# Where the low parts of two mixers' weights are computed, and where a softmax is scaled: VectorE and GpSimd change work

## The chip, the cores and the metric

The kernel runs on one core of a Trainium2 chip. The metric is the device time of one execution in microseconds (us). The matrix engine is called TensorE or PE, its weight loads PEld, VectorE DVE, ScalarE ACT, GpSimd POOL, and SyncE (which only issues DMAs here) SP. The granted clock is the share of TensorE's full speed that the chip allowed in a stretch; the two levels of the clock are 1.2 and 2.4 GHz.

## The reference

Two layers over 512 tokens of width 1024, float32. Layer 0 mixes tokens with two kinds of softmax attention side by side (a dilated window attention with 12 heads whose groups are combined, and a latent attention with 12 heads); layer 1 with a state-space recurrence (16 heads, in chunks of 128 tokens) beside a stick-breaking attention of 8 heads. Each is followed by a gated feed-forward block.

```python
def reference(x, positions, ...):
    for i in range(DEPTH):                       # DEPTH = 2, x is [1, 512, 1024]
        h = rmsnorm(x, mix_norms[i])
        if i % 2 == 0:
            x = x + even_mixer(h, positions, *mixers[i])
        else:
            x = x + odd_mixer(h, *mixers[i])
        x = x + conv_ffn(rmsnorm(x, ffn_norms[i]), *ffns[i])
    return rmsnorm(x, final_norm)

# in even_mixer, for every head and block of 128 queries
probs = jax.nn.softmax(jnp.where(causal, scores, -jnp.inf), axis=-1)
...
return jnp.einsum('bhqk,bkhd->bqhd', probs.astype(v.dtype), v)

def conv_ffn(h, w_gate, w_up, conv_w, conv_b, w_down):      # 1024 -> 2816 -> 1024
    gate = causal_dwconv(h @ w_gate, conv_w, conv_b)
    return (jax.nn.silu(gate) * (h @ w_up)) @ w_down
```

## The kernel before

Features lie on the partitions and the 512 tokens along the free dimension. TensorE multiplies in a rounded float32 format, so each float32 operand is split into a high part (the rounded copy) and a low part (what the rounding left), and a product is three matmuls: high by high, high by low, low by high.

**The weights.** They stream from memory in chunks of 128 partitions by up to 1024 columns. `wchunk` (L209 to L218) does one chunk: a DMA issued by SP into `wraw` (two buffers), the high part `whi` by ACT (L215), and the low part `wlo` = `wraw` - `whi` (L217), two buffers each. Unless its argument `eng` names an engine, L217 runs on GpSimd. `wstack` (L220 to L234) does the same for narrow weights, its low part at L233. The first two chunks are written out in `build` (L383). A buffer comes free when TensorE has multiplied with the chunk that was in it.

**The stages.** `build` runs four phases one after the other: mixer 0 (`even_mixer`), the feed-forward block 0, mixer 1 (`odd_mixer`: the state-space part `ssd`, then the stick-breaking part), the feed-forward block 1 with the final norm. The work that depends only on weights (projections) is cut into pieces by a `Stream`, and the pieces are put between the steps of the heads, so that TensorE has something to do while VectorE and ScalarE work on a head. TensorE takes its instructions in the order of the program; for the other engines a scheduler fixes the order when the kernel is built. Each engine then takes its own instructions strictly in that order.

**A head of mixer 0.** Per block of queries, TensorE writes the scores `s`, then `softmax` takes the maximum (L572, VectorE), the exponential with its sum (L575, ACT), the reciprocal `rl` of the sum (L576, VectorE) and multiplies by it (L577, VectorE; blocks of 128 to 512 keys, 64 in all). TensorE transposes the result (`t`), which is again split (`pth` on ACT, `ptl` on VectorE, L595 and L948), and multiplies it with the values (`o`). Before the heads, queries and keys are rotated (`rot`, `sw`, L726 to L731), split (`qk`, L261) or, for the latent attention, computed from the latents (`lat`, low part `ll`, L693; keys `knp` with low part `kl`, L850 and L868).

**The start.** The squares of x are computed on ACT and GpSimd (`sq`, L648) and added on VectorE (L652), between the first weights.

**The state-space part.** `run_conv` convolves a projection (`gt`, `cv`, L1144); `prepare` (L1260 to L1280) multiplies x by the time step (`xd`, L1269, alternately on GpSimd and VectorE), splits it (`xdt`, L1274), applies the skip term and the decay on GpSimd (L1277, L1279); `cdec` (L1258) is the decay of a chunk; `weights` computes a head's matrix and splits it (`sg`, L1328; `mh`, L261), and `apply` multiplies.

## Time and profile before

| | us |
|---|---|
| time, median of 3 runs | 1495.36 (1494.40 to 1495.47) |
| span of the profiled execution | 1491.7 |
| median less that span | 3.7 |
| PE busy | 1423.6 |
| PEld busy (beside PE) | 1158.3 |
| DVE busy | 874.7 |
| POOL busy | 697.1 |
| ACT busy | 658.0 |

The span is the time from the first to the last instruction in the profile of one execution; the time that is measured around an execution is some microseconds longer. TensorE is busy for 95% of the span, and its busy time includes matmuls that run at the low clock. The five stages of the span are mixer 0 (0 to 347 us), feed-forward 0 (347 to 712), the state-space part of mixer 1 (712 to 935), its stick-breaking part (935 to 1117), and feed-forward 1 with the end (1117 to 1492).

### The profile page before, as it was taken

Reading aid. Unit: us, or ns where it says so; the run is one execution under the profiler, and the core shown is the slowest. Engines: PE = TensorE matmul, PEld = TensorE weight load, DVE = VectorE, ACT = ScalarE, POOL = GpSimd, SP = SyncE. Lnnn points to the kernel's source line nnn. Section 1 sums busy time; section 2 is a strip of 40 time slices with the busy share of each in tenths; the row PEclk is TensorE's granted clock in tenths of the full one; section 3 lists DMA queues with packets and bytes.
Section 4 is the critical chain, followed back from the end, with each engine's and each line's share of the span. In section 5 each row is a group of like instructions: output and inputs, shape, how many; then the busy total and the mean of one; then the engine's idle time right before and its main releaser. Section 6 shows DMA issues by size and latency. Waiting matters only on the chain.

```text
span 1491.7 us, 18087 instructions
## 1 busy us (share of the span) xinstructions
PE 1423.6 (95%) x6842; PEld 1158.3 (78%) x6842; DVE 874.7 (59%) x1332; ACT 658.0 (44%) x1071; POOL 697.1 (47%) x405
## 2 busy tenths in 40 slices
PE   7989999999999999999988898999999999999997
PEld 5777778787888888888866667777888888888886
DVE  7888678736555555121788987678436555553123
ACT  4456456534433333232565465567444333333232
POOL 3633334133655555444335641466555555555441
PEclk8999999999999999999999999999999999999999
DMA  4321122122332233333222011111132233323332
GB/s 149 110 67 55 60 66 69 38 66 85 93 95 97 99 99 95 92 103 92 76 70 71 29 58 43 45 58 43 40 115 87 99 100 99 99 93 98 90 104 96
DMA packets 40006, 120.80 MB, mean 81 GB/s; under 512 B 5232, under 2 KB 8560, under 8 KB 39920
## 3 DMA queue, kind: packets, MB, share of 16 engines
q1 hardware_dynamic: 38160, 117.92, 25.1%
q10 hardware_dynamic: 1760, 1.73, 0.4%
q8 instruction: 54, 0.88, 0.2%
q14 instruction: 32, 0.26, 0.1%
HBM read 114.39 MB, written 2.10 MB: 78 GB/s over the span
## 4 chain that ended last, share of the span: by engine, by line
PE 77%; DVE 16%; ACT 3%; issue 3%; DMA 1%; POOL 0%; DVEq 0%; SPq 0%; ACTq 0%; POOLq 0%
PE proj L109 47%; PE o L109 19%; PE z L109 5%; PE s L109 3%; DVE cv L1144 2%; PE t L112 2%; PE t L109 1%; DVE mh L261 1%; DVE kl L868 1%; ACT whi L215 1%; DVE sg L1328 1%; DVE s L577 1%; DVE ptl L595 0%; DVE xe L261 0%; DVE s L572 0%
## 5 line engine op out<-in xcount | busy, mean ns | idle before, releaser
L217 POOL TENSOR_TENSOR wlo<-wraw,whi 128x1024 fp32r<-128x1024 f32 (+3 forms) x215 | 500.1, 2326 | 545.0 <-ACT whi L215 545.0
L215 ACT ACTIVATE whi<-wraw 128x1024 fp32r<-128x1024 f32 (+3 forms) x219 | 222.0, 1015 | 368.4 <-PE proj L109 320.4
L109 PE MATMUL proj<-xh,whi 128*128 128x512 f32 x844 | 348.5, 413 | 8.1 <-ACT xh L326 6.1
L109 PE MATMUL proj<-xh,wlo 128*128 128x512 f32 x844 | 336.8, 399 | 3.5 <-DVE wlo L383 3.3
L109 PE MATMUL proj<-xl,whi 128*128 128x512 f32 x844 | 336.6, 399 | 0.6 <-DVE xl L327 0.6
L109 PE MATMUL proj<-act,whi 128*128 128x512 f32 (+1 forms) x748 | 219.3, 377 | 0.0
L109 PEld LDWEIGHTS proj<-xh,whi 128*128 128x128 f32 x844 | 162.9, 193 | 45.5 <-ACT xh L326 8.8
L109 PEld LDWEIGHTS proj<-xh,wlo 128*128 128x128 f32 x844 | 162.4, 192 | 40.2 <-DVE wlo L383 3.7
L109 PEld LDWEIGHTS proj<-xl,whi 128*128 128x128 f32 x844 | 163.0, 193 | 30.8 <-DVE xl L327 2.3
L109 PEld LDWEIGHTS proj<-act,whi 128*128 128x128 f32 x748 | 137.6, 188 | 25.8
L109 PE MATMUL o<-xh,wlo 128*128 128x512 f32 x368 | 143.4, 390 | 0.0
L109 PE MATMUL o<-xh,whi 128*128 128x512 f32 x368 | 143.3, 389 | 0.0
L109 PE MATMUL o<-xl,whi 128*128 128x512 f32 x368 | 143.2, 389 | 0.0
L109 PE MATMUL proj<-act,wlo 128*128 128x512 f32 (+1 forms) x374 | 140.8, 376 | 0.0
L362 DVE TENSOR_TENSOR x<-x,proj 128x512 f32<-128x512 f32 x31 | 21.2, 685 | 177.2 <-PE proj L109 177.2
L515 DVE SCALAR_TENSOR_TENSOR cv<-gt,cols,cv 128x511 f32<-128x511 f32 x44 | 94.3, 2147 | 35.9 <-ACT cv L514 35.9
L519 POOL TENSOR_TENSOR sl<-sl,rsr 128x512 f32<-128x512 f32 x44 | 57.8, 1313 | 94.2 <-ACT sl L518 94.2
L524 DVE TENSOR_TENSOR up<-sl,o 128x512 f32<-128x512 f32 x44 | 30.3, 688 | 91.8 <-POOL sl L519 91.8
L518 ACT ACTIVATE sl<-cv 128x512 f32<-128x512 f32 x44 | 27.8, 631 | 127.3 <-DVE cv L516 127.3
L261 DVE TENSOR_TENSOR act<-up,act 128x512 fp32r<-128x512 f32 x44 | 63.2, 1436 | 29.3 <-ACT act L260 29.3
L109 PEld LDWEIGHTS proj<-act,wlo 128*128 128x128 f32 x374 | 70.4, 188 | 12.9
L109 PEld LDWEIGHTS o<-xh,wlo 128*128 128x128 f32 x368 | 69.1, 188 | 14.4
(302 smaller groups left out, 2232.4 us busy)
## 6 DMA issues: line engine op xcount, KB each, us to landing
wraw<-in_g SPq DMA_DIRECT2D x44, 512.0 KB, 3.5
wraw<-in_u SPq DMA_DIRECT2D x44, 512.0 KB, 3.4
wraw<-in_d SPq DMA_DIRECT2D x32, 448.0 KB, 3.2
wraw<-in_wqk SPq DMA_DIRECT2D x20, 512.0 KB, 3.5
wraw<-in_d SPq DMA_DIRECT2D x17, 512.0 KB, 3.5
wraw<-in_wx SPq DMA_DIRECT2D x12, 512.0 KB, 3.5
wraw<-in_wv SPq DMA_DIRECT2D x10, 512.0 KB, 3.5
wraw<-in_wz SPq DMA_DIRECT2D x8, 512.0 KB, 3.4
```

The costliest lines, as they stand in the source:

```text
L109: return self._put(self.b.nc.tensor.matmul(*args, **kw))
L112: return self._put(self.b.nc.tensor.transpose(*args))
L215: nc.scalar.activation(hi[:, :n], raw[:, :n], AF.Copy)
L217: (eng or nc.gpsimd).tensor_tensor(lo[:, :n], raw[:, :n], hi[:, :n].bitcast(F32), op=ALU.subtract)
L261: nc.vector.tensor_tensor(lo, src, hi.bitcast(F32), op=ALU.subtract)
L362: self.nc.vector.tensor_tensor(self.x[m], self.x[m], ps, op=ALU.add)
L515: nc.vector.scalar_tensor_tensor(c[:, 1:], gt[:, : T - 1], col_(1), c[:, 1:], op0=ALU.mult, op1=ALU.add)
L518: nc.scalar.activation(s, c, AF.Silu)
L519: nc.gpsimd.tensor_tensor(s, s, r, op=ALU.mult)
L524: nc.vector.tensor_tensor(u, s, pu, op=ALU.mult)
L577: nc.vector.tensor_scalar(t, t, rl, None, op0=ALU.mult)
L1144: nc.vector.scalar_tensor_tensor(c[:, d:], gt[:, : T - d], col_(j), c[:, d:], op0=ALU.mult, op1=ALU.add)
```

## The change

Two edits. In both mixers the low parts of the weights (L217, L233) are computed by VectorE, in both feed-forward blocks by GpSimd as before: an attribute `self.lo` holds the engine, and `build` sets it ahead of each phase. And in `softmax` the multiplication by 1/l is GpSimd's. The lines of the changed kernel behind `build`'s first phase carry numbers that are higher by five.

```diff
@@ wchunk
         lo = self.wp.tile([P, 1024], F32R, tag="wlo", name=self.nm("wlo"))
-        (eng or nc.gpsimd).tensor_tensor(lo[:, :n], raw[:, :n], hi[:, :n].bitcast(F32), op=ALU.subtract)
+        (eng or self.lo).tensor_tensor(lo[:, :n], raw[:, :n], hi[:, :n].bitcast(F32), op=ALU.subtract)
         return hi, lo
@@ wstack
-        nc.gpsimd.tensor_tensor(w[:, :, l0:l1], raw, w[:, :, a:b].bitcast(F32), op=ALU.subtract)
+        self.lo.tensor_tensor(w[:, :, l0:l1], raw, w[:, :, a:b].bitcast(F32), op=ALU.subtract)
         return w
@@ build
+        self.lo = nc.vector
         with self.phase("l0", s=2, t=2, o=2) as pool:
             self.even_mixer(pool)
+        self.lo = nc.gpsimd
         with self.phase("f0", t=2, o=2) as pool:
...
+        self.lo = nc.vector
         with self.tc.tile_pool(name="l1", bufs=1) as pool:
             self.odd_mixer(pool)
+        self.lo = nc.gpsimd
         with self.phase("f1", t=2, o=2) as pool:
@@ softmax
         nc.vector.reciprocal(rl, l)
-        nc.vector.tensor_scalar(t, t, rl, None, op0=ALU.mult)
+        nc.gpsimd.tensor_scalar(t, t, rl, None, op0=ALU.mult)
         return t
```

Over the whole program 82 low parts go from GpSimd's row to VectorE's: in mixer 0 20 of 1024 columns, 8 of 896, 6 of 768 and one stack of 512; in mixer 1 34 of 1024, 8 of 768, 4 of 512 and one stack of 128. The 64 multiplications of the softmax go the other way: 24 of 512 columns, 16 of 384, 12 of 256 and 12 of 128. The rows of TensorE and of SP stay as they were. Three places show what VectorE's and GpSimd's rows look like.

**The start of mixer 0.** VectorE's row before, from the sums of squares to the first angles:

```order
L664 CAST posf<-posi 128x512
L652 TENSOR_TENSOR sq_150<-sq_150,sq_166 128x512
L383 TENSOR_TENSOR wlo_79<-wraw_77,whi_78 128x512
L652 TENSOR_TENSOR sq_152<-sq_152,sq_163 128x512
L546 TENSOR_SCALAR ang_256<-posf,freq 128x512
L652 TENSOR_TENSOR sq_152<-sq_152,sq_169 128x512
L547 TENSOR_SCALAR angk_257<-ang_256 128x512
```

and now, with a second piece from the steps of the reciprocal root (`rst`, `rsy`):

```order
L657 TENSOR_TENSOR sq_150<-sq_150,sq_166 128x512
L383 TENSOR_TENSOR wlo_79<-wraw_77,whi_78 128x512
L657 TENSOR_TENSOR sq_152<-sq_152,sq_163 128x512
L551 TENSOR_SCALAR ang_256<-posf,freq 128x512
L217 TENSOR_TENSOR wlo_176<-wraw_172,whi_174 128x1024
L657 TENSOR_TENSOR sq_152<-sq_152,sq_169 128x512
...
L272 TENSOR_TENSOR rst_240<-rsy_239 128x4
L273 SCALAR_TENSOR_TENSOR rst_240<-rst_240,rsv_237 128x4
L274 SCALAR_TENSOR_TENSOR rsy_239<-rst_240,rsy_239 128x4
L217 TENSOR_TENSOR wlo_390<-wraw_386,whi_388 128x1024
L272 TENSOR_TENSOR rst_240<-rsy_239 128x4
```

The low part `wlo_176` now stands ahead of the last of these sums, and `wlo_390` among the steps of the reciprocal root. On GpSimd both stood behind the squares.

**The first scores of a head.** GpSimd's row before, from the first weight of this stretch to the second rotation's end:

```order
L217 TENSOR_TENSOR wlo_538<-wraw_534,whi_536 128x768
L730 TENSOR_TENSOR sw_496<-sw_496,sin 128x512
L731 TENSOR_TENSOR rot_497<-rot_497,sw_496 128x512
L217 TENSOR_TENSOR wlo_590<-wraw_586,whi_588 128x1024
L730 TENSOR_TENSOR sw_576<-sw_576,sin 128x512
L731 TENSOR_TENSOR rot_577<-rot_577,sw_576 128x512
L217 TENSOR_TENSOR wlo_645<-wraw_641,whi_643 128x768
L217 TENSOR_TENSOR wlo_747<-wraw_743,whi_745 128x1024
L730 TENSOR_TENSOR sw_733<-sw_733,sin 128x512
```

and now:

```order
L735 TENSOR_TENSOR sw_496<-sw_496,sin 128x512
L736 TENSOR_TENSOR rot_497<-rot_497,sw_496 128x512
L735 TENSOR_TENSOR sw_576<-sw_576,sin 128x512
L736 TENSOR_TENSOR rot_577<-rot_577,sw_576 128x512
L582 TENSOR_SCALAR s_126_656<-s_126_656,st_655 128x512
L582 TENSOR_SCALAR s_129_670<-s_129_670,st_669 128x384
L582 TENSOR_SCALAR s_132_684<-s_132_684,st_683 128x256
L582 TENSOR_SCALAR s_135_698<-s_135_698,st_697 128x128
L735 TENSOR_TENSOR sw_733<-sw_733,sin 128x512
```

The four low parts have left, and the multiplications of the softmax stand between two of the rotations (`sw`, `rot`). VectorE's row now, in the same stretch:

```order
L774 TENSOR_TENSOR rt_611<-proj_604,qt_520 128x512
L873 TENSOR_TENSOR kl_568<-knp_602,kh_567 64x512
L873 TENSOR_TENSOR kl_572<-knp_602,kh_571 64x512
L628 TENSOR_TENSOR v_622<-t_617,v_622 128x8x64
L774 TENSOR_TENSOR rt_632<-proj_625,qt_524 128x512
L261 TENSOR_TENSOR qk_614<-rt_611,qk_613 128x512
L217 TENSOR_TENSOR wlo_645<-wraw_641,whi_643 128x768
L261 TENSOR_TENSOR qk_635<-rt_632,qk_634 128x512
L577 ISA s_126_656,st_655<-s_651,masks 128x512
```

Here `wlo_645` has come in between the low parts `qk` of the first head's queries and keys, ahead of the first softmax (the row that reads the scores `s_651`).

**The values of the state-space part.** VectorE's row before, from the last convolution on:

```order
L1138 TENSOR_TENSOR gt_6699<-proj_6668,rsr_6080 128x512
L1269 TENSOR_TENSOR xd_6759<-xs_6087,tok 128x512
L1144 SCALAR_TENSOR_TENSOR cv_6701<-gt_6699,cols,cv_6701 128x511
L1144 SCALAR_TENSOR_TENSOR cv_6701<-gt_6699,cols,cv_6701 128x510
L1144 SCALAR_TENSOR_TENSOR cv_6701<-gt_6699,cols,cv_6701 128x509
L1258 COPY cdec<-s_6739 128x48
L1274 TENSOR_TENSOR xdt_6747<-xd_6745,xdt_6747 128x4x64
L1274 TENSOR_TENSOR xdt_6750<-xd_6745,xdt_6750 128x4x64
```

and now:

```order
L1143 TENSOR_TENSOR gt_6699<-proj_6668,rsr_6080 128x512
L217 TENSOR_TENSOR wlo_6718<-wraw_6714,whi_6716 128x1024
L1274 TENSOR_TENSOR xd_6759<-xs_6087,tok 128x512
L1149 SCALAR_TENSOR_TENSOR cv_6701<-gt_6699,cols,cv_6701 128x511
L1279 TENSOR_TENSOR xdt_6747<-xd_6745,xdt_6747 128x4x64
L1279 TENSOR_TENSOR xdt_6750<-xd_6745,xdt_6750 128x4x64
L1149 SCALAR_TENSOR_TENSOR cv_6701<-gt_6699,cols,cv_6701 128x510
L1279 TENSOR_TENSOR xdt_6761<-xd_6759,xdt_6761 128x4x64
L1279 TENSOR_TENSOR xdt_6764<-xd_6759,xdt_6764 128x4x64
L1263 COPY cdec<-s_6739 128x48
```

GpSimd's row at the same place before:

```order
L217 TENSOR_TENSOR wlo_6718<-wraw_6714,whi_6716 128x1024
L1269 TENSOR_TENSOR xd_6745<-xs_6087,tok 128x512
L1277 TENSOR_TENSOR xs_6087<-xs_6087,dbc 128x512 x2
L1279 TENSOR_TENSOR xd_6745<-xd_6745,tok 128x512
L1279 TENSOR_TENSOR xd_6759<-xd_6759,tok 128x512
L217 TENSOR_TENSOR wlo_6840<-wraw_6836,whi_6838 128x1024
L1269 TENSOR_TENSOR xd_6773<-xs_6087,tok 128x512
```

and now:

```order
L1274 TENSOR_TENSOR xd_6745<-xs_6087,tok 128x512
L1282 TENSOR_TENSOR xs_6087<-xs_6087,dbc 128x512 x2
L1284 TENSOR_TENSOR xd_6745<-xd_6745,tok 128x512
L1284 TENSOR_TENSOR xd_6759<-xd_6759,tok 128x512
L1274 TENSOR_TENSOR xd_6773<-xs_6087,tok 128x512
```

On VectorE the low part `wlo_6718` stands ahead of `xd_6759`, and `cdec`, which stood ahead of the four `xdt`, now stands behind them and ahead of the convolution's last step. On GpSimd nothing stands ahead of `xd_6745` and `xd_6773` but work on the same values.

## Rows read from the trace of the kernel before

**Rows 1.** The profile's page: the line of the span, the busy time of each engine (us, share of the span, instructions), and each engine's share of the chain that ended last.

```profile
span 1491.7 us, 18087 instructions
PE 1423.6 (95%) x6842; PEld 1158.3 (78%) x6842; DVE 874.7 (59%) x1332; ACT 658.0 (44%) x1071; POOL 697.1 (47%) x405
...
PE 77%; DVE 16%; ACT 3%; issue 3%; DMA 1%; POOL 0%; DVEq 0%; SPq 0%; ACTq 0%; POOLq 0%
```

**Rows 2.** Busy time by stage; a row is a stretch in us from the span's start (mixer 0; FFN 0; the state-space part of mixer 1; its stick-breaking part). Columns: length, the busy time of PE, PEld, DVE, ACT and POOL with the number of instructions, the granted clock of TensorE as a share of full speed, the share of the DMA engines, GB/s.

```profile
0.00:347.00 347.00, 319.77 (x1793) 257.32 (x1794) 254.42 (x575) 181.65 (x357) 129.90 (x73) 0.96 0.24 76
347.00:712.00 365.00, 364.14 (x1620) 301.31 (x1619) 162.63 (x155) 125.95 (x157) 187.57 (x91) 1.00 0.31 96
712.00:935.00 223.00, 197.71 (x931) 153.66 (x930) 183.48 (x258) 119.67 (x222) 96.54 (x56) 0.95 0.17 55
935.00:1117.00 182.00, 176.94 (x810) 140.77 (x810) 108.47 (x162) 101.57 (x173) 102.72 (x98) 0.98 0.19 59
```

**Rows 3.** Groups of instructions of ScalarE, VectorE and GpSimd by line and shape (the first with four shapes together) over the whole span: count | busy us, mean ns of one | idle time before them and what ended most of it.

```profile
L215 ACT ACTIVATE whi<-wraw 128x1024 fp32r<-128x1024 f32 (+3 forms) x219 | 222.0, 1015 | 368.4 <-PE proj L109 320.4
...
L217 DVE TENSOR_TENSOR wlo<-wraw,whi 128x1024 fp32r<-128x1024 f32 x2 | 2.4, 1224 | 7.7 <-ACT whi L215 7.6
L868 DVE TENSOR_TENSOR kl<-knp,kh 64x512 fp32r<-64x512 f32 x12 | 15.4, 1279 | 0.3
...
L217 POOL TENSOR_TENSOR wlo<-wraw,whi 128x1024 fp32r<-128x1024 f32 x159 | 388.0, 2441 | 351.4 <-ACT whi L215 351.4
L730 POOL TENSOR_TENSOR sw<-sw,sin 128x512 f32<-128x512 f32 x12 | 16.7, 1390 | 29.8 <-DMA sw<-raw 20.0 <-DVE ptl L948 2.6 <-DVE st L572 2.6
L1486 POOL TENSOR_SCALAR_AFFINE_SELECT ab<-ab 128x256 f32<-128x256 f32 x16 | 7.8, 488 | 15.1 <-DVE ab L1507 7.6 <-ACT ab L1531 7.5
```

**Rows 4.** The instructions of line 577 alone (the softmax's multiplication by 1/l) in the stretch of mixer 0, with the columns of rows 2; they stand in the third busy time, that of VectorE.

```profile
0.00:347.00 347.00, 32.62 (x64) 0.96 0.24 76
```

**Rows 5.** The start of mixer 0 in order of time: start us, length us, engine, line, operation, shape, count, and in brackets the idle time before it and who ended it. One row of GpSimd, two of VectorE, two of TensorE, then a stretch with the columns of rows 2.

```profile
17.69 2.81 POOL L217 TENSOR_TENSOR wlo<-wraw,whi 128x1024 fp32r<-128x1024 f32 x1
18.20 2.85 DVE L652 TENSOR_TENSOR sq<-sq,sq 128x512 f32<-128x512 f32 x1
21.92 0.68 DVE L383 TENSOR_TENSOR wlo<-wraw,whi 128x512 fp32r<-128x512 f32 x1
22.65 0.50 PE L109 MATMUL proj<-xh,wlo 128*128 128x512 f32 x1 [3.27 <-DVE wlo L383]
25.81 3.41 PE L109 MATMUL t<-ones,sq 128*128 128x1 f32 x16
24.00:36.00 12.00, 12.00 (x42) 10.15 (x41) 9.13 (x30) 4.84 (x7) 3.09 (x1) 0.57 0.28 106
```

**Rows 6.** Up to the scores of the first head, in the same columns: GpSimd, VectorE, TensorE, and a stretch. The row at 118.94 is an undisturbed instruction of the kind of that at 71.61.

```profile
58.62 1.82 POOL L217 TENSOR_TENSOR wlo<-wraw,whi 128x768 fp32r<-128x768 f32 x1 [2.22 <-ACT whi L215]
45.68 2.89 DVE L693 SCALAR_TENSOR_TENSOR ll<-lat,cols,lh 128x512 fp32r<-128x512 f32 x1
58.76 2.23 DVE L838 TENSOR_TENSOR kpe<-cs,rsr 32x512 f32<-32x512 f32 x1
71.61 3.54 DVE L868 TENSOR_TENSOR kl<-knp,kh 64x512 fp32r<-64x512 f32 x2
118.94 0.68 DVE L868 TENSOR_TENSOR kl<-knp,kh 64x512 fp32r<-64x512 f32 x1
77.42 0.50 PE L109 MATMUL s<-kh,qk 128*128 128x512 f32 x1 [3.56 <-DVE qk L261]
78.00:84.00 6.00, 6.00 (x25) 5.15 (x23) 3.69 (x18) 3.05 (x9) 0.00 (x0) 0.72 0.23 83
```

**Rows 7.** Between the heads of mixer 0, in the same columns: the longest wait of TensorE there, and two stretches.

```profile
128.81 0.33 PE L109 MATMUL o<-ptl,v 128*128 128x128 f32 x1 [3.05 <-DVE ptl L595]
126.00:138.00 12.00, 9.19 (x43) 8.10 (x44) 9.67 (x32) 5.35 (x14) 1.60 (x1) 0.86 0.13 44
276.00:288.00 12.00, 10.71 (x87) 8.11 (x84) 9.11 (x18) 4.58 (x11) 1.84 (x1) 0.72 0.11 38
```

**Rows 8.** Groups of VectorE and of GpSimd in 712 to 935 us alone, columns as in rows 3.

```profile
L261 DVE TENSOR_TENSOR mh<-sg,mh 128x512 fp32r<-128x512 f32 x16 | 17.9, 1119 | 1.2 <-ACT mh L260 1.0
L1328 DVE TENSOR_TENSOR sg<-sg,cb 128x512 f32<-128x512 f32 x16 | 17.9, 1116 | 2.3 <-ACT sg L1325 2.3
L1144 DVE SCALAR_TENSOR_TENSOR cv<-gt,cols,cv 128x511 f32<-128x511 f32 x12 | 15.8, 1318 | 9.5 <-ACT cv L1141 9.5
L217 POOL TENSOR_TENSOR wlo<-wraw,whi 128x1024 fp32r<-128x1024 f32 x24 | 59.4, 2474 | 94.2 <-ACT whi L215 94.2
```

**Rows 9.** Where the values of the state-space part are prepared, in order of time, columns as in rows 5: GpSimd, VectorE, TensorE, and a stretch.

```profile
804.04 1.49 POOL L1269 TENSOR_TENSOR xd<-xs,tok 128x512 f32<-128x512 f32 x1
813.65 2.46 DVE L261 TENSOR_TENSOR xe<-xd,xe 128x512 fp32r<-128x512 f32 x1 [0.71 <-ACT xe L260]
809.14 0.54 PE L109 MATMUL s<-cm,idb 128*128 128x512 bf16 x1 [2.48 <-DVE cdec L1258]
822.65 0.50 PE L109 MATMUL o<-xdt,mh 128*128 128x128 f32 x2 [3.88 <-DVE xdt L1274]
825.62 0.69 PE L109 MATMUL o<-xdt,mh 128*128 128x128 f32 x2 [2.46 <-DVE xdt L1274]
800.00:830.00 30.00, 19.48 (x73) 13.28 (x72) 26.74 (x29) 15.95 (x32) 20.68 (x15) 0.83 0.13 42
```


## The prediction

> **What bounds the kernel.** I read the page's busy times and the chain first: TensorE is busy for 95% of the span, and the chain that ended last runs through it for 77% and through VectorE for 16%; GpSimd is hardly on it, although it works for 697 us [rows 1]. So a shorter GpSimd row is worth nothing by itself; what counts is what it does to VectorE. The table by stage then shows where the missing 5% lies: feed-forward 0 leaves TensorE idle for 0.9 us of 365, mixer 0 for 27 of 347, the state-space part for 25 of 223, the stick-breaking part for 5 of 182 [rows 2]. The change touches exactly these mixers. VectorE is at 73% and 82% in the first two, at 60% in the third. A wait there costs twice: after several of the waits TensorE's granted clock lies between its two levels, 0.57 after the first one, 0.72 and 0.86 after later ones [rows 5 to 7].
>
> Last I read, in order of time, what VectorE does ahead of each wait. Where it stands beside a running GpSimd instruction, an instruction with two inputs from SBUF is long: `kpe` starts 0.14 us behind a low part on GpSimd and takes 2.23 us, to 0.55 us past that one's end; an undisturbed one of its kind (64x512 instead of 32x512) takes 0.68 [rows 6]. At the start the third sum of squares takes 2.85 us beside a low part of 2.81, and the low part TensorE waits for comes behind it [rows 5]. This pattern is the reason why work on GpSimd costs VectorE time.
>
> The Trainium skill has the rule (SBUF — State Buffer, Who interferes with whom): VectorE and GpSimd share a pair of ports as an exclusive lock, and who comes first keeps it for the whole instruction. The trace agrees (2.23 against 0.68 us); by this rule a low part on VectorE can also be the one that is locked out, which is a rival below.
>
> **Prices.** A low part of 1024 columns takes 2.44 us on GpSimd and 1.22 on VectorE [rows 3], one of 512 on VectorE 0.68 [rows 5]; between them 768 is about 0.95 and 896 about 1.09. So VectorE gets in mixer 0 20 x 1.22 + 8 x 1.09 + 6 x 0.95 + 0.68 = 39.6 us, in mixer 1 34 x 1.22 + 8 x 0.95 + 4 x 0.68 + some 0.3 = 52. It loses the 64 multiplications, 32.6 us, all in mixer 0 [rows 4]. GpSimd loses about twice these 92 us. What a multiplication by a column of numbers takes on GpSimd no row shows. Bounds: 0.49 us for any size, as an operation with one input of 256 columns (31 us in all), and 1.39 per 512 columns, as one with two inputs (63 us) [rows 3]. It has one wide input, so it is nearer to the first; I take 40 us, 0.62 each, against 0.51 on VectorE [rows 4]. That and the handing over lie in a chain of a head, but behind other pieces on TensorE, so they cost little unless GpSimd is late.
>
> The Trainium skill (GPSIMD Engine Reference, Engine selection) puts elementwise work on VectorE and GpSimd at half its speed with two inputs, about equal with one. The trace agrees for two inputs (2.44 to 1.22); by it the low parts move the right way and the multiplication gains nothing by its own length.
>
> **The sum, place by place.**
>
> *The start.* `wlo_176` no longer runs on GpSimd beside the third sum; this falls from 2.85 to about 0.68, and `wlo_79`, for which TensorE waits 3.27 us, comes 2.2 us earlier [rows 5]. The wait left, 1.1 us, is short enough that I take the clock to stay up. From 24 to 36 us it stood at 0.57: 12 x 0.43 = 5.2 us lost if all were wide matmuls; without the 3.4 us of one-column ones, 3.7 [rows 5]. Against it `wlo_390` now stands among the steps of the reciprocal root that all latents wait for: +1.2. Together -4.7, bounds -7.4 (2.2 + 5.2, `wlo_390` hidden) and -1.0 (the clock falls all the same).
>
> *Up to the first scores.* TensorE waits 3.56 us for `qk`, and 6 us at 0.72 follow (1.7 us lost). Ahead of it VectorE lost 2.2 us on `ll`, 1.55 on `kpe`, 2.2 on the pair of `kl` at 71.61, each against 0.68 [rows 6]: 5.9. Five low parts come in (three of 1024, two of 768, the last directly ahead of the second `qk`): 5.6 us, of which the 27% of time in which VectorE idles in this stage [rows 2] hide a part; 4.1 remain. -5.9 + 4.1 - 1.7 = -3.5, bounds -7.6 (all hidden) and +4 (GpSimd's rotations keep the stalls up).
>
> *Between the heads.* VectorE loses the 32.6 us, and of the stalls on the ten other `kl` about 10 x 0.6 = 6 (mean 1.28 against 0.68) [rows 3, 6]. It gets 39.6 less 3.1 (start) less 5.6 less 4.4 (four behind the last head, where TensorE has only matmuls with weights to do) = 26.5, and about 3 us of new stalls beside the multiplications on GpSimd (my choice: 24 wide ones, each catching a VectorE instruction for 0.12 us on average). Balance -9.1 us of VectorE. Its waits reach TensorE only in part: the longest is 3.05 us for `ptl`, with a clock of 0.86 behind it, and 0.72 for 12 us near 280 [rows 7]. I take less than half: -4, bounds -14 (all of it, with the 1.7 and 3.4 us of clock) and +4 (half of 24 low parts hold a head's step for 0.35 us).
>
> *The state-space part.* VectorE's three groups `mh`, `sg`, `cv` are 0.44, 0.44 and 0.64 us above 0.68 each, 16, 16 and 12 times: 22 us [rows 6, 8]. Taking as much again for the other kinds, 44 us are stalls beside GpSimd; the low parts are 59.4 of its 96.5 us [rows 2, 8], so 27 go. In come 24 x 1.22 = 29. VectorE's load is even; the gain is in what GpSimd hands on: `xd` at 804.04 came directly behind a low part, and another stood ahead of the next one. TensorE waits 2.48, 3.88 and 2.46 us here for `cdec` and `xdt`, and 30 us run at 0.83, 5.1 lost [rows 9]. `xe` at 813.65, 2.46 us long, loses its neighbour too. Against it `wlo_6718` and `wlo_6840` now take 2.4 us of VectorE, and `cdec` comes behind four `xdt`. I take 4 us of the 8.8 and 2 of the clock: -6, bounds -13.9 (all) and +5 (two low parts and a late `cdec`).
>
> *The stick-breaking part.* VectorE idles for 40%, TensorE waits for 5 us in all [rows 2]: -0.5, bounds 3 either way.
>
> *The new wait.* A low part at the head of VectorE's row waits there for ACT's high part (1.0 us long, itself held by TensorE's release of the buffer), and every step behind it waits too; on GpSimd that cost nothing. The two rows of before on VectorE waited 3.8 us each for it, the upper bound; the lower is nothing [rows 3]. I take 82 x 1.0 us x 0.3 (as often as it comes too early) x a quarter (what reaches TensorE past VectorE's idle time) = +6.2; these two shares are chosen, not read.
>
> Sum: -4.7 - 3.5 - 4 - 6 - 0.5 + 6.2 = -12.5. 1491.7 - 12.5 = 1479.2 for the span, and with the 3.7 us between the profiled span and the median of the runs **1483 us**.
>
> **Rivals.**
> - *Everything arrives* (0.06): no low part waits, and the waits at 800 to 830 us vanish: -6.2 and -7.9 more, 1469 us. Against it: `cdec` is later in VectorE's row.
> - *The lock changes sides* (0.16): the low parts on VectorE, two inputs each, wait for GpSimd's rest. GpSimd keeps some 90 us of mixer 0 (130 - 80 + 40), 26% of it, and 37 us of the state-space part, 17% [rows 2, 8]. 35 x 0.26 x 0.7 + 24 x 0.17 x 0.7 = 9 us more on VectorE, half of it on the path: 1487.5.
> - *VectorE was not what counted* (0.10): the balances fall into its idle time, the start's 4.7 us are paid back by the new wait: 1495, no change.
> - *The low parts hold VectorE's row* (0.18), on the other side: all 82 stand for the full 1.0 us, a quarter reaches TensorE, 20.5 instead of 6.2 us, and the held steps are those of the heads, so that the 7.5 us gained there go too: 1505. It decides from 0.23 us per low part on TensorE's path on (18.7 us, the sum without the new wait). For it speak the 3.8 us of the two rows; against it, that these two stand where VectorE has little else to do [rows 3].
> - That the change does not do what it says is excluded: VectorE's row holds the 82 low parts.
>
> **Numbers.** The forecast has 0.50, its own range 1475 to 1491. From 1466 to 1500 the best of the first rival and the last rival's centre are left out, about 2 in 10. A measurement of this kernel can tell 0.2% (3 us) from no change. Faster: 0.06 + 0.50 + 0.14 of the lock's 0.16 = 0.70; same: 0.02 + 0.10 = 0.12; slower 0.18.
>
> **What would show it.** Right: the third sum below 1 us, TensorE's wait for `wlo_79` near 1 us and full clock from 24 to 36 us; `kl` near 0.7; a multiplication of 512 on GpSimd at 0.7; shorter waits at the three places near 810 to 826 us; VectorE's busy time near 900 us, GpSimd's near 550. Wrong: much idle time of VectorE ended by ACT's `whi` ahead of L217, low parts on VectorE far above 1.22 us, or transposes in mixer 0 that wait for GpSimd's multiplication.

## The result and the profile after

The changed kernel takes 1475.93 us (median of 5 runs, 1473.35 to 1480.33) against 1494.40 us for the kernel before (median of 5): a ratio of 0.9886 with a 95% interval of 0.9865 to 0.9908, so 1.1% faster. The forecast was 1483 us, its own range 1475 to 1491, the wide one 1466 to 1500. The direction and the ranges held, the first of them only just; 12.5 us less were forecast, and 18.5 less came. Most parts of the sum did not hold: mixer 0 gave less than was forecast and mixer 1 more, and these errors cancelled in part. Of the runs below, one of `lo_mixer1` (1693.64 us, its mean granted clock 0.784 where the others had 0.980 to 0.986) is left out as slow.

The page of the changed kernel, with the lines that answer to [rows 1]:

```profile
span 1475.5 us, 18223 instructions
PE 1412.1 (96%) x6842; PEld 1151.4 (78%) x6842; DVE 874.6 (59%) x1350; ACT 658.3 (45%) x1071; POOL 598.1 (41%) x387
...
PE 79%; DVE 13%; ACT 3%; issue 3%; DMA 1%; POOL 1%; DVEq 0%; SPq 0%; ACTq 0%; POOLq 0%
```

VectorE is as busy as before, 874.6 us (forecast: near 900), GpSimd has 598 us instead of 697 (forecast: near 550), and VectorE's share of the chain fell from 16% to 13%. The same stretches as in [rows 2] (the later ones hold work that has moved forward by up to 16 us):

```profile
0.00:347.00 347.00, 315.98 (x1793) 253.89 (x1794) 247.34 (x547) 180.99 (x357) 128.35 (x102) 0.97 0.24 76
712.00:935.00 223.00, 205.12 (x978) 160.02 (x977) 185.69 (x292) 129.32 (x238) 43.09 (x35) 0.97 0.19 59
935.00:1117.00 182.00, 178.07 (x843) 144.12 (x843) 124.52 (x195) 100.06 (x168) 65.98 (x75) 1.00 0.21 64
```

GpSimd's time in the state-space part is less than half, 43 us instead of 97, and VectorE's time there is as before although it took over the low parts. The groups that answer to [rows 3] and [rows 8], over the whole span:

```profile
L217 DVE TENSOR_TENSOR wlo<-wraw,whi 128x1024 fp32r<-128x1024 f32 x56 | 70.4, 1258 | 14.9 <-ACT whi L215 14.7
L873 DVE TENSOR_TENSOR kl<-knp,kh 64x512 fp32r<-64x512 f32 x12 | 10.4, 868 | 0.2
L1333 DVE TENSOR_TENSOR sg<-sg,cb 128x512 f32<-128x512 f32 x16 | 13.2, 825 | 3.3 <-ACT sg L1330 3.3
L261 DVE TENSOR_TENSOR mh<-sg,mh 128x512 fp32r<-128x512 f32 x16 | 13.0, 810 | 0.7 <-ACT mh L260 0.7
L1149 DVE SCALAR_TENSOR_TENSOR cv<-gt,cols,cv 128x511 f32<-128x511 f32 x12 | 9.7, 808 | 0.9 <-ACT cv L1146 0.9
...
L582 POOL TENSOR_SCALAR s<-s,st 128x512 f32<-128x512 f32 x24 | 39.0, 1626 | 81.2 <-DVE st L581 73.3 <-PE t L112 5.0 <-DVE st L579 2.9
L582 POOL TENSOR_SCALAR s<-s,st 128x128 f32<-128x128 f32 x12 | 7.2, 603 | 5.4 <-DVE st L581 5.4
L1274 POOL TENSOR_TENSOR xd<-xs,tok 128x512 f32<-128x512 f32 x4 | 5.4, 1356 | 37.5 <-ACT tok L1255 34.9 <-DVE xe L261 1.9 <-DVE xdt L1279 0.8
```

`kl` fell from 1.28 to 0.87 us, `sg` and `mh` from 1.12 to about 0.82, `cv` from 1.32 to 0.81: these instructions no longer stand beside the low parts on GpSimd. A low part on VectorE costs nearly what was expected, 1.26 us on average, so it is seldom held up by GpSimd's rest. VectorE waited 14.9 us for high parts ahead of the 56 of 1024 columns; 7.7 of these belong to the two that were VectorE's before, as they did then [rows 3]. GpSimd's multiplications are far off the forecast: 1.63 us for 512 columns and 0.60 for 128, where 0.62 was taken as the average. And `xd` on GpSimd now waits for its own input (37.5 us, nearly all ahead of the first) instead of standing behind weights.

**Where the time went.** TensorE executes the same instructions in the same order in all kernels of this study, so the same instruction can be found in two traces, and the difference of its starts is TensorE's lead over the kernel before. The table cuts TensorE's row at its first instruction and at those that start at 50, 80, 300, 712, 935 and 1100 us in the trace of before. Each cell has three numbers worked out from the traces: the lead won in the piece, the time in which no matmul ran (waits), and the time at the lower clock level, all in us; 300 to 712 us, where nothing but a stray drop of the clock changes the lead, is left out. A lead is about the change of the waits plus half the change of the time at the low clock.

| kernel | 0 to 50 | 50 to 80 | 80 to 300 (heads) | 712 to 935 (state space) | 935 to 1100 (stick) |
|---|---|---|---|---|---|
| before | 0 / 3.9 / 10.2 | 0 / 4.5 / 4.7 | 0 / 11.3 / 15.8 | 0 / 25.3 / 23.9 | 0 / 5.1 / 6.8 |
| the change | 5.9 / 2.5 / 0 | -0.5 / 3.2 / 10.2 | -5.4 / 17.8 / 13.7 | 12.4 / 17.2 / 13.7 | 4.2 / 4.6 / 0 |
| the change again (`change_again`) | 6.3 / 2.8 / 0 | 1.2 / 4.4 / 2.9 | -2.8 / 19.6 / 3.9 | 11.4 / 17.3 / 17.1 | 2.7 / 4.6 / 3.4 |
| `lo_only` | 6.5 / 3.1 / 0 | 0.2 / 4.6 / 5.1 | -9.9 / 18.5 / 22.2 | 12.7 / 16.4 / 17.1 | 4.2 / 4.6 / 0 |
| `mul_only` | 3.2 / 4.7 / 3.4 | -3.9 / 7.7 / 6.8 | 2.4 / 13.1 / 6.8 | -0.1 / 25.4 / 23.9 | -0.1 / 5.1 / 6.8 |
| `lo_mixer1` | -1.2 / 4.8 / 13.7 | -1.2 / 4.0 / 9.5 | 1.6 / 11.4 / 11.0 | 12.5 / 16.4 / 17.1 | 4.1 / 4.6 / 0 |
| `mul_act` | 6.2 / 3.2 / 0 | 0.2 / 4.6 / 4.8 | -4.8 / 17.8 / 12.2 | 12.4 / 16.4 / 17.1 | 4.2 / 4.6 / 0 |
| `lo_start` | 5.6 / 2.8 / 0 | 0.0 / 4.8 / 5.0 | 2.5 / 11.5 / 8.7 | 12.3 / 16.4 / 17.1 | 4.2 / 4.6 / 0 |
| `lo_start_again` | 6.7 / 2.7 / 0 | -0.3 / 4.1 / 7.8 | 2.2 / 11.5 / 9.2 | 13.5 / 16.4 / 13.7 | 4.2 / 4.6 / 0 |
| `lo_start_mul` | 5.3 / 3.2 / 0 | -2.6 / 4.7 / 12.0 | 1.1 / 13.2 / 11.9 | 12.3 / 16.4 / 17.1 | 4.3 / 4.6 / 0 |
| `lo_start_ssd` | 6.3 / 3.0 / 0 | 0.7 / 4.7 / 3.4 | 2.8 / 11.0 / 10.2 | 12.6 / 16.4 / 17.1 | 2.5 / 5.3 / 0 |
| `extra_write` | 5.8 / 2.7 / 0 | -0.4 / 4.6 / 6.2 | -5.6 / 17.8 / 14.3 | 6.3 / 21.3 / 20.5 | 2.2 / 5.9 / 0 |
| `extra_read` | 6.2 / 3.1 / 0 | 1.0 / 3.2 / 6.8 | -4.7 / 18.4 / 10.2 | -24.6 / 40.5 / 51.2 | -10.1 / 12.0 / 6.8 |

The row of the change tells the story: 6 us won at the start, all of it lost again up to the end of the heads, 16.6 us won in mixer 1. The rows of one and the same piece show how much to trust a number: the waits repeat within 2 us from execution to execution, the clock's drops do not (13.7 and 3.9 us between the heads for the same kernel). So below I go by the waits where they are there, and count a lead that comes from the clock only where it repeats in all the kernels that share the piece.

### The profile page after: what moved, and what is told of

Its sections match the earlier page's. It is cut to its first block, busy times and chain, and to the rows that moved or that the text cites. A ratio compares the mean times of both kernels' runs of the same rounds, so it can differ in the third digit from the quotient of the medians.

```text
span 1475.5 us, 18223 instructions
## 1 busy us (share of the span) xinstructions
PE 1412.1 (96%) x6842; PEld 1151.4 (78%) x6842; DVE 874.6 (59%) x1350; ACT 658.3 (45%) x1071; POOL 598.1 (41%) x387
## 4 chain that ended last, share of the span: by engine, by line
PE 79%; DVE 13%; ACT 3%; issue 3%; DMA 1%; POOL 1%; DVEq 0%; SPq 0%; ACTq 0%; POOLq 0%
PE proj L109 50%; PE o L109 19%; PE z L109 5%; PE s L109 3%; DVE wlo L217 2%; PE t L112 2%; PE t L109 1%; ACT whi L215 1%; DVE xdt L1279 1%; DVE cv L1149 1%; DVE sg L1333 1%; DVE mh L261 0%; DMA x<-in_x 0%; DVE xs L1348 0%; DVE xl L327 0%
## 5 line engine op out<-in xcount | busy, mean ns | idle before, releaser
L217 POOL TENSOR_TENSOR wlo<-wraw,whi 128x1024 fp32r<-128x1024 f32 (+1 forms) x135 | 315.2, 2335 | 322.1 <-ACT whi L215 322.1
L582 POOL TENSOR_SCALAR s<-s,st 128x512 f32<-128x512 f32 (+1 forms) x64 | 80.6, 1264 | 114.9 <-DVE st L581 97.9
L362 DVE TENSOR_TENSOR x<-x,proj 128x512 f32<-128x512 f32 x31 | 21.3, 686 | 173.6 <-PE proj L109 173.4
L217 DVE TENSOR_TENSOR wlo<-wraw,whi 128x1024 fp32r<-128x1024 f32 (+3 forms) x84 | 98.0, 1167 | 29.8 <-ACT whi L215 29.3
```

Source lines behind the costliest of these rows:

```text
L217: (eng or self.lo).tensor_tensor(lo[:, :n], raw[:, :n], hi[:, :n].bitcast(F32), op=ALU.subtract)
L362: self.nc.vector.tensor_tensor(self.x[m], self.x[m], ps, op=ALU.add)
L582: nc.gpsimd.tensor_scalar(t, t, rl, None, op0=ALU.mult)
```

## The experiments

The theories ahead of the first runs: A, the multiplication on GpSimd lengthens a head's chain and ate the lead; B, VectorE's load decides between the heads, and giving the multiplication away is what kept mixer 0 even.

**The two halves of the change apart (`lo_only`, `mul_only`).** Edits to the changed kernel:

```diff
 # lo_only, in softmax
-        nc.gpsimd.tensor_scalar(t, t, rl, None, op0=ALU.mult)
+        nc.vector.tensor_scalar(t, t, rl, None, op0=ALU.mult)
 # mul_only, in build, ahead of both mixers
-        self.lo = nc.vector
+        self.lo = nc.gpsimd
```

> Only the low parts move to VectorE; the multiplication by 1/l stays there. Theory A (the multiplication on GpSimd, 1.55 us for 512 columns in the trace of the change against 0.53 on VectorE, lengthens the heads' chains and ate the lead of mixer 0): TensorE's lead over the kernel before stays near 6 to 10 us at 300 us, and with the 16.6 us of mixer 1 the time is about 1470 us. Theory B (VectorE's load decides between the heads): with 32.6 us more on VectorE the lead at 300 us falls below zero, to about -8, and the time is about 1484 us.

> Only the multiplication by 1/l moves to GpSimd; all low parts stay on GpSimd. Mixer 1 is as before, so the time tells mixer 0 alone. Theory A: slower than before, by about 5 us, 1499 us, with transposes of the softmax that wait for GpSimd's multiplication. Theory B: VectorE is 32.6 us lighter, faster by 5 to 10 us, about 1487 us.

Measured on one chip: `lo_only` 0.9919 (0.9894 to 0.9945), 1479.92 us; `mul_only` 1.0014 (1.0001 to 1.0028), 1493.04 us. Theory A falls with `lo_only`: without the multiplication on GpSimd the lead is not kept, it is lost more completely (-3.2 us at 300 us), and the waits between the heads are 18.5 us as against 17.8 in the change. Theory B does not fare well either: `mul_only` makes VectorE lighter by 32.6 us and wins nothing; its waits between the heads are 1.8 us longer than before. The two longest in the list of TensorE's waits from 80 to 300 us of that kernel (waiting line, the engine waited for, its line, us in total, times, longest):

```profile
PE t L112 <- DVE ptl L953: 5.1, 1, 5.1
PE t L112 <- POOL s L582: 3.7, 5, 1.8
```

The second row is a new kind: transposes that wait for the multiplication on GpSimd, five times, 3.7 us. They are the price of the slow multiplication; the waits as a whole grew by half of that.

**Mixer 1 alone, and the multiplication on a third engine (`lo_mixer1`, `mul_act`).**

```diff
 # lo_mixer1: as lo_only, and in build, ahead of mixer 0
-        self.lo = nc.vector
+        self.lo = nc.gpsimd
 # mul_act: the change, but in softmax
-        nc.gpsimd.tensor_scalar(t, t, rl, None, op0=ALU.mult)
+        nc.scalar.activation(t, t, AF.Copy, scale=rl)
```

> Only the low parts of mixer 1 move to VectorE; mixer 0 is as before, the multiplication by 1/l on VectorE. If the gain of the change lies in mixer 1 alone (lead 0.2 us at 300 us, 16.8 at the end), the time is that of the change, about 1478 us (1494.4 less 16.6). If part of it hung on what mixer 0 leaves behind, it is above 1481 us.

> The low parts move as in the change, the multiplication by 1/l goes to ScalarE instead of GpSimd (a copy scaled by a column). Theory A: the head's chain has no GpSimd link, the lead of mixer 0 stays near 6 to 10 us, about 1469 us. Theory B: VectorE as light as in the change, so the same 1476 us as the change or better. Rival: ScalarE, with 35 us more in mixer 0, delays exponentials and high parts of weights, and the lead at 300 us is below zero: above 1478 us.

Measured: `lo_mixer1` 0.9894 (0.9868 to 0.9920), 1475.23 us; `mul_act` 0.9899 (0.9879 to 0.9918), 1476.18 us. The low parts of mixer 1 by themselves give the whole gain of the change, as expected. In `mul_act` the head's chain has no GpSimd link, VectorE is as light as in the change, and the waits between the heads are 17.8 us all the same. The time is the one that theory B gave, but B has fallen with `mul_only`; and ScalarE's delays, the rival named there, can't be what the waits of the other two kernels come from. So it is not the multiplication, wherever it runs. The three kernels so far with the low parts of mixer 0 on VectorE (the change, `lo_only`, `mul_act`) wait 17.8 to 18.5 us between the heads, the three with them on GpSimd (before, `mul_only`, `lo_mixer1`) 11.3 to 13.1.

**The low parts on VectorE only up to the heads (`lo_start`, `lo_start_mul`).** Theory C: a low part of 1.2 us in VectorE's row holds back the split that TensorE waits for. Edit, in `even_mixer`, where the heads are set up; `lo_start` has the multiplication on VectorE, `lo_start_mul` on GpSimd:

```diff
+        self.lo = nc.gpsimd
         heads = [mla_head(pr, e) for pr in range(6) for e in range(2)]
```

> In mixer 0 only the low parts up to the heads (start, latents, first rotations) are VectorE's, between the heads they are GpSimd's again; in mixer 1 VectorE's; the multiplication by 1/l on VectorE as before. Theory C (between the heads a low part on VectorE holds back the split that TensorE waits for, and that ate the start's lead): the lead of 6 to 7 us at 60 us stays until 300 us, and with the 16.3 us of mixer 1 the time is 22 to 23 us under the kernel before, a ratio of 0.985. Rival D (the lead is lost whatever is done, because TensorE, when it comes earlier, only waits longer for the same chain of a head): the lead at 300 us is near 0, ratio 0.989.

> As the run before it, with the multiplication by 1/l on GpSimd. Theory C: the multiplication alone gave 1.7 us of lead in mixer 0 (run with the multiplication alone), so ratio 0.984. If the multiplication only pays where VectorE also has the low parts, no better than without it: 0.985 or above.

Measured: `lo_start` 0.9839 (0.9809 to 0.9870), 1469.29 us; `lo_start_mul` 0.9847 (0.9818 to 0.9875), 1468.68 us. Theory C holds, rival D falls: the waits between the heads are back at 11.5 us and the lead of the start stays to the end. The added line is the only difference between `lo_only` and `lo_start`, and the only one between the change and `lo_start_mul`: it takes the waits between the heads from 18.5 to 11.5 us and from 17.8 to 13.2. A lighter VectorE is not what counts: in 0 to 347 us it is busy for 259.9 us in `lo_start`, more than the 247.3 of the change, and TensorE waits less. The multiplication on GpSimd brings nothing that can be measured on top; its waits are 13.2 us against 11.5.

The place shows it best. VectorE and TensorE in the changed kernel, at two of the waits (start us, length us, then the instruction, in brackets the wait and who ended it):

```profile
185.01 1.21 DVE L217 TENSOR_TENSOR wlo<-wraw,whi 128x1024 fp32r<-128x1024 f32 x1
186.14 0.55 DVE L953 TENSOR_TENSOR ptl<-t,pth 128x384 fp32r<-128x384 f32 x1
186.84 0.63 PE L112 MATMUL t<-ident,s 128*128 128x128 f32 x4 [2.95 <-DVE ptl L953]
...
234.20 1.22 DVE L217 TENSOR_TENSOR wlo<-wraw,whi 128x1024 fp32r<-128x1024 f32 x1
235.34 0.68 DVE L760 TENSOR_TENSOR vt<-proj,rsr 128x512 f32<-128x512 f32 x1
236.07 0.50 PE L109 MATMUL proj<-lh,whi 128*128 128x512 f32 x1 [1.43 <-DVE vt L760]
```

and the first of these places in `lo_start`:

```profile
183.93 0.68 DVE L774 TENSOR_TENSOR rt<-proj,qt 128x512 f32<-128x512 f32 x1
184.65 0.56 DVE L953 TENSOR_TENSOR ptl<-t,pth 128x384 fp32r<-128x384 f32 x1
185.27 1.06 PE L112 MATMUL t<-ident,s 128*128 128x128 f32 x4 [2.03 <-DVE ptl L953]
```

In `lo_start` `ptl` comes directly behind `rt` (184.65), and TensorE waits 2.03 us for it. In the change `wlo` stands between the two; VectorE does not idle, it works on `wlo` for 1.21 us, and TensorE waits 2.95. At 234.20 the same happens ahead of `vt`. From the lists of TensorE's waits from 80 to 300 us, of the change and then of `lo_start`:

```profile
PE o L109 <- DVE ptl L600: 5.0, 4, 1.8
PE proj L109 <- DVE vt L760: 3.3, 4, 1.4
PE t L112 <- DVE ptl L953: 2.9, 1, 2.9
```

```profile
PE o L109 <- DVE ptl L600: 3.9, 3, 3.1
PE t L112 <- DVE ptl L953: 2.0, 1, 2.0
...
PE proj L109 <- DVE vt L760: 1.1, 3, 0.6
```

TensorE waits longer in the change for each of the three: for `vt`, one of the values' steps, 3.3 us instead of 1.1.

**What helped in mixer 1 (`extra_read`, `extra_write`).** Both are the change, and put work back on GpSimd in mixer 1 that no computation needs; a flag `self.extra` is set for that phase alone:

```diff
 # extra_read, in wchunk behind the low part
+        if self.extra:
+            nc.gpsimd.tensor_tensor(raw[:, :n], raw[:, :n], hi[:, :n].bitcast(F32), op=ALU.subtract)
 # extra_write
+        if self.extra:
+            for _ in range(2):
+                nc.gpsimd.memset(raw[:, :n], 0.0)
```

> The change, and in mixer 1 GpSimd does 46 subtractions more, of the same size as the low parts it gave up, into the buffer of the raw weight after VectorE has read it; no engine waits for their result, only the next load waits for the buffer. Lock theory (VectorE's instructions with two inputs stand still beside a GpSimd instruction that reads SBUF): the groups mh and sg go from 0.81 and 0.83 us back to about 1.1, and most of the 16.6 us of mixer 1 is lost, ratio 0.996 or above. Rival (what helped was that GpSimd's own work, xd and the like, came earlier): mh and sg stay near 0.8, xd comes late, ratio about 0.995 too. Rival (it was the better order of VectorE's row alone): ratio as in the change, 0.989.

> As the run before it, but GpSimd fills the dead raw buffer with zeros twice in place of the subtraction: about the same time on GpSimd (two times 1.06 us), reading nothing. Lock theory: mh and sg stay near 0.8 us, and the gain of mixer 1 stays, ratio 0.990. Theory of the late GpSimd: as bad as with the subtraction, 0.995.

Measured: `extra_read` 1.0239 (1.0210 to 1.0269), 1526.52 us; `extra_write` 0.9964 (0.9943 to 0.9986), 1485.57 us. The groups of VectorE in the state-space part and GpSimd's added work, of `extra_read`, which is later there (712 to 960 us; columns as in rows 3):

```profile
L1335 DVE TENSOR_TENSOR sg<-sg,cb 128x512 f32<-128x512 f32 x16 | 19.2, 1202 | 3.8 <-ACT sg L1332 3.6
L263 DVE TENSOR_TENSOR mh<-sg,mh 128x512 fp32r<-128x512 f32 x16 | 13.2, 823 | 0.8 <-ACT mh L262 0.7
L1151 DVE SCALAR_TENSOR_TENSOR cv<-gt,cols,cv 128x511 f32<-128x511 f32 x12 | 13.2, 1102 | 0.9 <-ACT cv L1148 0.9
L219 POOL TENSOR_TENSOR wraw<-wraw,whi 128x1024 f32<-128x1024 f32 x23 | 62.0, 2696 | 114.5 <-DVE wlo L217 94.0 <-issue 20.5
```

and of `extra_write` (712 to 935 us):

```profile
L1336 DVE TENSOR_TENSOR sg<-sg,cb 128x512 f32<-128x512 f32 x16 | 12.8, 797 | 3.4 <-ACT sg L1333 3.4
L264 DVE TENSOR_TENSOR mh<-sg,mh 128x512 fp32r<-128x512 f32 x16 | 13.6, 848 | 0.8 <-ACT mh L263 0.7
L1152 DVE SCALAR_TENSOR_TENSOR cv<-gt,cols,cv 128x511 f32<-128x511 f32 x12 | 8.9, 743 | 0.9 <-ACT cv L1149 0.9
L220 POOL MEMSET wraw<- 128x1024 f32 x46 | 44.0, 956 | 110.7 <-DVE wlo L217 109.6
```

The added work is 62 us of GpSimd in the one kernel and 44 in the other. With the reading work `sg` goes to 1.20 us and `cv` to 1.10; with the writing work they stay at 0.80 and 0.74. So an instruction of VectorE with two inputs from SBUF is long beside a GpSimd instruction that reads SBUF, and not beside one that only writes. `mh` missed the expectation, it stayed at 0.82 and 0.85. The trace has the reason: only one of its 16 instructions in `extra_read` ran beside an added subtraction, and the nine that ran beside no GpSimd instruction took 0.67 to 0.69 us each. In `extra_write` the `sg` and `mh` that ran beside the zeros alone took 0.68 to 0.69. The Trainium skill (SBUF — State Buffer, Who interferes with whom) states both halves of this: contention with a GpSimd instruction that reads SBUF, none with one that only writes it. `sg` and `cv` in these two runs agree with it.

But `extra_write`, where the zeros lengthen neither `sg` nor `cv`, also lost half of the 16.6 us of mixer 1 (waits 21.3 us in the state-space part, against 17.2 in the change and 25.3 before). The lock theory by itself gave 0.990 and has missed; 0.9964 is near the 0.995 of the theory of the late GpSimd. The third, that of VectorE's order (0.989), is not put to the test, because the added work changed that order, as the next rows show. TensorE's waits for `xdt` in the state-space part, of before and then of `extra_write`, tell where it went; the change has none:

```profile
PE o L109 <- DVE xdt L1274: 6.3, 2, 3.9
PE o L109 <- DVE xdt L1282: 4.3, 2, 2.5
```

GpSimd's second `xd` starts at 812.70 us in `extra_write`, directly behind a filling with zeros that had waited for VectorE's low part; in the change it starts at 807.15. But VectorE's row is another one too: its own second `xd` stands behind two `mh` there, ahead of which it stood in the change, and starts at 816.37 instead of 810.50. So the late values are back, and whether GpSimd's order or VectorE's brought them, these runs don't tell apart; nor do they give what share of the change's gain in mixer 1 is the stalls that are gone. That the buffer of the raw weight comes free later, which both runs bring with them, shows little: VectorE idles 2.9 us for high parts of 1024 columns there, 2.3 in the change. The loss in `extra_read` is far above what the change had won (a lead of -24.6 us in the state-space part); beyond the stalls I can't divide it.

**On one chip, and the stick-breaking part (`change_again`, `lo_start_again`, `lo_start_ssd`).** The first two are the change and `lo_start` unaltered; the third is `lo_start` with one line ahead of the stick-breaking phase:

```diff
+        self.lo = nc.gpsimd
         with self.phase("stick", z=4, t=1, o=1) as sub:
```

> The change itself once more, on the chip of the next two runs, so that these can be set beside it: ratio to the kernel before 0.987 to 0.991, lead of TensorE near 0 at 300 us and 16 to 17 us at 1100 us.

> VectorE's low parts in mixer 0 only up to the heads, multiplication by 1/l on VectorE, mixer 1 as in the change. If theory C holds, it is 5 to 8 us below the change on the same chip (ratio to before 0.982 to 0.986); if the first run of it was luck, it is within 2 us of the change.

> As the run before it, but in the stick-breaking part of mixer 1 the low parts stay on GpSimd. The prediction put that part at -0.5 us; the traces show 3.6 us of lead at its start, where a drop of TensorE's clock at 949 us is gone. If the low parts of this part made it, the lead ends near 19 us instead of 23, and the time is some 3.5 us above the run before it; if it came with the state-space part's end, the time is the same within 1 us; if the moved low parts cost something there, as between the heads of mixer 0, it is faster.

Measured: the change 0.9904 (0.9875 to 0.9934), 1477.48 us; `lo_start` 0.9844 (0.9816 to 0.9872), 1469.38 us; `lo_start_ssd` 0.9862 (0.9835 to 0.9890), 1472.39 us. `lo_start` is 8.1 us under the change, the intervals do not touch, and it beats both kernels. The change's ratio came as expected, its leads did not: 4.7 us at 300 us and 18.8 at 1100, because the clock fell less between the heads (3.9 us at the low level); the waits there are again long, 19.6 us. In the stick-breaking part the low parts on VectorE are worth some 0.7 us of waits (4.6 against 5.3) and a lead of 1.7; the medians differ by 3.0, with intervals that overlap, so none of the three outcomes that were written down is clearly met. Most of the lead of 4.2 us there (2.5 of it also in `lo_start_ssd`) is the drop of the clock near 949 us that is gone; since it is gone in `lo_start_ssd` as well, the low parts of this part are not what removed it.

## Why the prediction was right in the sum, and where its steps were wrong

**The sum.** That it fits is in part luck. The new wait was spread evenly over the 82 low parts, so 2.6 us of it belong to mixer 0 and 3.6 to mixer 1. With these, mixer 0 was forecast at -9.6 us and mixer 1 at -2.9. In the two traces of the change mixer 0 came to 0.0 and -4.7, mixer 1 to -16.6 and -14.1: too little in the one and too much in the other.

**The start (-4.7 forecast; 5.9 and 6.3 us won).** Right in mechanism. The profile after, VectorE, TensorE and a stretch in the columns of [rows 5]:

```profile
15.58 3.57 DVE L657 TENSOR_TENSOR sq<-sq,sq 128x512 f32<-128x512 f32 x3
20.75 0.50 PE L109 MATMUL proj<-xh,wlo 128*128 128x512 f32 x1 [1.07 <-DVE wlo L383]
24.00:36.00 12.00, 11.41 (x58) 9.10 (x57) 10.05 (x31) 6.37 (x11) 0.26 (x1) 1.00 0.37 129
```

The three sums take 3.57 us together, where they took 5.75 before (the third alone 2.85, [rows 5]): 2.2 us less, as worked out. TensorE waits 1.07 us for `wlo_79` (forecast 1.1) and the clock stays up from 24 to 36 us. The 10.2 us at half clock before are gone, 5.1 us, where I had taken 3.7. How long the clock stays down with the old start differs by execution: 10.2 us before, 13.7 in `lo_mixer1` and 3.4 in `mul_only`, which won 3.2 us here mainly by that. But with the new start it is nothing in all ten traces, so the gain is real, and its size uncertain by a few microseconds.

**Up to the first scores (-3.5 forecast; about 0).** Wrong. The rows of VectorE, GpSimd and TensorE say why:

```profile
52.61 0.96 DVE L217 TENSOR_TENSOR wlo<-wraw,whi 128x768 fp32r<-128x768 f32 x1 [3.50 <-ACT whi L215]
57.83 1.76 DVE L836 TENSOR_TENSOR qt<-cs,rsr 32x512 f32<-32x512 f32 x1
59.62 1.65 DVE L844 TENSOR_TENSOR kpe<-pes,kpe 64x512 f32<-64x512 f32 x1
57.76 1.29 POOL L735 TENSOR_TENSOR sw<-sw,sin 128x512 f32<-128x512 f32 x1 [7.24 <-DMA sw<-raw]
59.12 1.59 POOL L736 TENSOR_TENSOR rot<-rot,sw 128x512 f32<-128x512 f32 x1
61.32 1.86 PE L109 MATMUL o<-kpe,fold 64*128 64x512 f32 x2 [2.14 <-DVE kpe L844]
72.58 0.50 PE L109 MATMUL s<-kh,qk 128*128 128x512 f32 x1 [1.03 <-DVE qk L261]
```

The low part of 768 columns stood at the head of VectorE's row for 3.50 us until its high part was there, with the steps of `kpe` behind it; and two of these then ran beside GpSimd's rotation, so that `qt` took 1.76 us instead of 0.68, and the last `kpe` 1.65, as it had before (1.67). TensorE waits 2.14 us for `kpe` instead of 0.60 (and the clock is at 0.50 from 62 to 66 us), and 1.03 instead of 3.56 for `qk` [rows 6]. Part of the stalls that I counted as removed stayed or came back with another partner: this is the upper bound's condition (GpSimd's rotations keep the stalls up), and the new wait in its pure form.

**Between the heads (-4 forecast; 2.8 and 5.4 us lost) and the new wait (+6.2).** The step that failed is that VectorE's balance (-9.1 us) reaches TensorE in part. VectorE did become lighter, 247 us instead of 254 in mixer 0 as a whole. TensorE's waits still grew by 6.5 us. What counts there isn't how much VectorE does but what stands ahead of the splits. That the new wait's +6.2 is near these 6.5 us is chance: it was meant for both mixers, and for another reason. VectorE's low parts from 80 to 300 us:

```profile
L217 DVE TENSOR_TENSOR wlo<-wraw,whi 128x1024 fp32r<-128x1024 f32 x14 | 18.5, 1319 | 3.8 <-ACT whi L215 3.8
L217 DVE TENSOR_TENSOR wlo<-wraw,whi 128x768 fp32r<-128x768 f32 x4 | 3.8, 955 | 0.5 <-ACT whi L215 0.4
L217 DVE TENSOR_TENSOR wlo<-wraw,whi 128x896 fp32r<-128x896 f32 x3 | 3.5, 1161 | 0.4 <-ACT whi L215 0.4
```

Ahead of these 21, VectorE idles for 4.7 us; on them it works for 25.8. So it does not mostly idle for a high part, it works for 1.2 us on a weight that nobody needs yet while TensorE needs `ptl` or `vt`. The sum had this work as load, in the balance, and not as a delay of the step behind it.

**The multiplication.** Mis-sized: 0.62 us each was taken, upper bound 63 us in all; it took 80.8 us in its four groups, 1.63 us for 512 columns, and an undisturbed one at 133 us 1.56. The nearest row was the wrong one: a row of 0.49 us for 256 columns of a selection does not price a multiplication by a column of numbers. It cost TensorE up to 1.8 us of waits, because other pieces cover most of it. On VectorE, before, the same 24 took a third of that:

```profile
L577 DVE TENSOR_SCALAR s<-s,st 128x512 f32<-128x512 f32 x24 | 12.8, 534 | 0.5
```

The Trainium skill (GPSIMD Engine Reference, Engine selection) has an operation with one input run on GpSimd at roughly line rate, where one with two is about twice as slow as on VectorE. That does not hold here: with one wide input it is 1.56 against 0.53 us.

**The state-space part (-6 forecast; 12.4 and 11.4 us won).** Right at the places that were named, half the size. The three waits of [rows 9] were to fall by 4 us; they are now these:

```profile
805.01 0.38 PE L109 MATMUL s<-cm,idb 128*128 128x512 bf16 x1 [1.07 <-DVE cdec L1263]
812.47 0.33 PE L109 MATMUL o<-xdt,mh 128*128 128x128 f32 x1 [1.20 <-ACT mh L260]
816.17 1.87 PE L109 MATMUL o<-xdt,mh 128*128 128x128 f32 x7 [3.37 <-DVE mh L261]
```

8.8 us have become 5.6, so 3.2 less, near the forecast, although the `xdt` waited for has become a `mh`. `cdec` did not come late. All together the waits in the stage fell by 8.1 us; the other 4.9 are at places that I had not counted at all, because I read only the longest: `bc` at 755 us, `xe`, `mh` at 915 and the many under a microsecond. So the term that was too small is these 4 us. The clock gave 3.4 to 5.1 us more, where 2 were taken. Of the 22 us of stalls in the three groups 16 are gone. The mechanism as forecast, values that GpSimd hands on earlier, fits `extra_write`, but is not shown apart from VectorE's new order.

**The stick-breaking part (-0.5 forecast; 4.2 and 2.7).** Its waits did fall by only 0.5 us. What was missed is the 6.8 us at the low clock from 949 us on, worth 3.4 us: the change's trace has none of it there, that of `change_again` half.

**The rivals.** The lock changing sides, 0.16: little, a low part on VectorE takes 1.26 instead of 1.22 us on average (1.32 between the heads, one of them 2.34). The low parts holding VectorE's row, 0.18: in mixer 0 they did, and cost 6.5 us of waits, but by their own length and not by standing for a high part; in mixer 1 the gain outweighed it. VectorE not being what counted, 0.10: no, the time fell. Everything arriving, 0.06: no, of the 8.8 us of waits at 800 to 830 us there are still 5.6.

## What to carry to other kernels

Ask of a piece of work not only which engine does it faster, but what stands behind it in that engine's row: moving the same 1.2 us low parts won 14 to 18 us in mixer 1, where VectorE was held up by GpSimd's reading and both engines shared a chain, and lost 6 us of waits where TensorE waits for VectorE's next short step. Set the engine by stage and measure each stage by the lead at the same instruction of the busiest engine; the version that does so here (VectorE up to the heads and in mixer 1, GpSimd between the heads) takes 1469 us, 8 less than the change on the same chip. Count all the waits of a stage, not the longest three, and take the clock as a bonus that differs from one execution to the next.

## What the runs showed of the hardware that was not expected

- A multiplication by a column of numbers on GpSimd takes 0.60 us for 128 and 1.56 for 512 columns undisturbed; on VectorE one of 512 averages 0.53 in the trace of before.
- VectorE's `sg` averages 1.20 us in the kernel with GpSimd's added reading work and 0.80 in the one with added writing work, although GpSimd is busy in both.
- For one and the same kernel, TensorE's time at the lower of its two clock levels between the heads was 13.7 us in one execution and 3.9 in another, with waits of 17.8 and 19.6 us.
